# Copying the first output gate out of PSUM, and tying two background steps to the product issued last

## The chip, the cores and the metric

The kernel runs on one core of a Trainium2 chip. The metric is the time on the device in microseconds (us); the reported time is the median of three runs. Next to it stands one execution that the hardware profiler recorded, from which all views of the trace come.

## The reference

One layer of a diffusion backbone, for 256 latent tokens and 256 context tokens of width 2048. Both pass a modulated RMS norm, then one wide input projection `w_in`, whose columns feed two token mixers: attention with 16 query heads on 4 key heads (with a norm and a rotary turn of queries and keys, and a sink), and gated linear attention (GLA) with 4 heads of value width 512. What matters for the change is the attention with its sink, the norm of the keys, and the output gate of the GLA:

```python
def attend_with_sink(parts, sink_g):
    sink_b = sink_g[None, :, :, None]
    m = sink_b
    for s, _ in parts:
        m = jnp.maximum(m, s.max(axis=-1))
    denom = jnp.exp(sink_b - m)
    ...
    for s, val in parts:
        p = jnp.exp(s - m[..., None])
        denom = denom + p.sum(axis=-1)
        o = jnp.einsum("bhgqk,bkhd->bqhgd", p, val.astype(jnp.float32))
        ...
    return out / jnp.transpose(denom, (0, 3, 1, 2))[..., None]
```

The four heads of the GLA's output are normed and multiplied with the SiLU of four blocks of 512 columns of the input projection (the "output gate", RB in the kernel). Both mixers are projected, merged by sigmoid gates (GA and GB), projected again and added to the stream; a gated convolutional FFN follows. All is computed in float32.

## The kernel before

**How a product is made.** Weights stream from HBM in tiles of 256 x 512 (`wload`, seven buffers, on SyncE's DMA queue). Each is split into a high part `whi` (a copy on ScalarE, ACT, into a rounded format, L220) and the rest `wlo` (a subtraction on VectorE, DVE, L221), three buffers of each. Every product is three matmuls on TensorE (PE): high x high, low x high, high x low. The activations are split the same way: `split` (L61 to L63) makes `hi` on ACT and `lo` on DVE. `mm` (L84) issues a matmul of the main stream and remembers it in `last[0]`; `last_lo[0]` is the last `wlo` subtraction. `proj_nat` runs over the rows of a weight block in steps of 256, 12 matmuls a step where two tiles of 128 tokens come out and 24 where four do, into banks of PSUM named `acc` (four banks), and calls `tick()` at the start of each step and `midway()` in the middle. Three more banks are of a kind `side` (names `pg`, `pS`, `ptp`, `poa`, `pto`), one is `main` (`ptk`, `ptq`).

**What sets the order.** The program is written in one stream, and a scheduler places each instruction on its engine's queue; at run time each engine takes its queue in order. Background work (norms, transposes, attention) is put in between by `defer(n, fn)`, which calls `fn` n ticks later, and by a generator `beside`, of which `tick` and `midway` advance a part. `in_order(a, b)` adds a dependency without a semaphore: the scheduler places b behind a in time, and at run time nobody waits for it.

**The first place (456 to 545 us in the trace).** The GLA's value columns of the third and fourth head are not multiplied directly with the tokens; `pair_values` first mixes the tokens. `natural(kp)` takes 256 columns of x and of the context in natural layout (tile `raw`, 128 x 4 x 256), scales them by the norm with four operations on DVE (L1144) with a row tile `rows`, adds the shift (two on POOL or DVE, L1149), splits them into `h0` or `h1` by the parity of kp, and calls `fetch(kp + 1)`, which loads x, context and `rows` of the next; `rows` has one buffer. `inner(kp)` multiplies `h0` or `h1` with the GLA's mixing tiles `ax` and `ac` into two `pg` banks (24 matmuls), and splits them into `h2` or `h3`. `outer(kp, i, w)` multiplies these with the weights. The loop runs inner(0); then natural(2), inner(1), outer(0); natural(3), inner(2), outer(1); and so on to kp = 7. natural(0) and natural(1) are deferred into the product GA before it. The norm and the rotary turn of the keys, `norm_rope(..., copied=True)`, four of them (`keys(i)`), are deferred by 10, 13, 16 and 19 ticks from there; the first step of each is the Square at L1106 on ACT, whose sums DVE takes at L1108. The rotary tables are multiplied by the norm's weights on POOL (L1093 and L1095) in the same stretch.

**The second place (700 to 800 us).** The output gate: `rb_block(j)` computes one block of 512 columns, and `rb_evac` evacuates its two banks with a Silu on ACT (L1336), multiplies it with the normed GLA output on DVE (L1339, L1340), and transposes it later. The attention of the last group of heads runs beside block 0: `attend` puts the scores into banks `pS`, takes exponentials on ACT (L1283), scales them on DVE (L1288), transposes them on PE (`ptp`), splits these (`pth`, `ptl`, L62 and L63) and multiplies them with the values (`poa`). Since exponential and Silu need different tables on ACT, each Silu is tied behind the last exponential, `exps[-1]`, by `in_order`, so that the table is loaded once. Block 2 writes into the banks that block 0 had.

Of the kernel before, what the change touches and what calls it, by code (L numbers as in the profile page):

```python
# [11 lines left out]
AF = mybir.ActivationFunctionType  # L12
# [20 lines left out]
def layer_kernel(ctx, tc, A, out):  # L33
    nc = tc.nc
    V, S, G, PE = nc.vector, nc.scalar, nc.gpsimd, nc.tensor
# [18 lines left out]
    def W2(tag, name, shape, dt=F32):  # L54
        return f2.tile(shape, dt, name=name, tag=tag, bufs=F2_BUFS[tag])
# [5 lines left out]
    def split(hi, lo, src):  # L61
        S.activation(hi, src, AF.Copy)  # L62
        return V.tensor_tensor(lo, src, hi.bitcast(F32), op=ALU.subtract).ins  # L63

    def in_order(*ins):

        for a, b in zip(ins, ins[1:]):
            tc.add_manual_dep(b, a.name, mybir.DependencyInfo(
                mybir.DependencyClass.NoSync, mybir.DependencyReason.DATA), reason="order")

    last, pin = [None], [None]
# [77 lines left out]
    def defer(n, fn):  # L149

        later.append([n, fn])
# [282 lines left out]
    def rms_scale(ss, n, shape):  # L434

        v = sm.tile(shape, F32, name="msq", tag="msq")
        r = sm.tile(shape, F32, name="rstd", tag="rstd")
        t = sm.tile(shape, F32, name="newt", tag="newt")
        V.tensor_scalar(v, ss, 1.0 / n, EPS, op0=ALU.mult, op1=ALU.add)
        S.activation(r, v, AF.Ln)  # L440
        S.activation(r, r, AF.Exp, scale=-0.5)
        V.tensor_tensor(t, r, r, op=ALU.mult)
        V.tensor_tensor(t, t, v, op=ALU.mult)
        V.tensor_scalar(t, t, -0.5, 1.5, op0=ALU.mult, op1=ALU.add)
        V.tensor_tensor(r, r, t, op=ALU.mult)
        return r
# [91 lines left out]
    def affine_shift(s, t0, n, behind=None):  # L538
        for kt in range(t0, t0 + n):
            xk = xr[2 * s + kt // 8][:, kt % 8, :]  # L540
            sh = shift1[:, s, kt:kt + 1]
            hi, lo = hh[kt // 4][:, s, kt % 4, :], hl[kt // 4][:, s, kt % 4, :]
            j = S.activation(hi, xk, AF.Identity, bias=sh).ins
            if behind is not None and kt == t0:
                in_order(behind, j)
            i = V.scalar_tensor_tensor(lo, xk, sh, hi.bitcast(F32), op0=ALU.add, op1=ALU.subtract).ins
        return i, j
# [50 lines left out]
    i, j = affine_shift(0, *groups[0])  # L598
# [3 lines left out]
    for j in range(2):  # L602
        proj_T(w_in, QB + j * 512, kts, [h_all(0)],
               lambda i, b, j=j: evicted.append(S.activation(qb0[2 * j + i], b, AF.Copy).ins), fresh=(j == 0))
# [28 lines left out]
    i, j = affine_shift(1, *groups[1])  # L633
# [341 lines left out]
    def v_block(c0, name, by_tile=False):  # L975
        vh, vl = M(name + "h", [P, 4, 512], F32R), M(name + "l", [P, 4, 512], F32R)
        proj_nat(w_in, 0, c0, ALL, h_xc, lambda i, b: split(vh[:, i, :], vl[:, i, :], b),
                 by_tile=by_tile)
        return vh, vl
# [19 lines left out]
    def with_gla(h, kb, block, extra=()):  # L999
        res, own = [], []  # L1000

        def level():
            if not own:
                own.append(gla_A(h, kb, qbt, *gates[h][0], res))
            next(own[0], None)

        this, following = lambda: gate(h), lambda: gate(h + 1)
        places = {i: [this] for i in ((0, 1, 2, 3) if h == 0 else (0, 1))}
        for i in (4, 6, 7, 8, 9, 10, 11, 12) if h == 0 else (2, 4, 5, 7, 8, 10, 11, 12):
            places[i] = [level]  # L1010
        places.update({13: [level], 14: [following], 15: [level]})
        places.setdefault(13 if h == 0 else 9, []).append(following)

        for i, fn in enumerate(extra):
            places.setdefault(11 + i, []).append(fn)

        def along():
            for i in range(16):
                for fn in places.get(i, ()):
                    fn()  # L1020
                yield

        beside[:] = [along(), 1.0, 0.0]
        v = block()
        for _ in beside[0]:
            pass
        beside.clear()
        return res, v
# [14 lines left out]
    def first_values(i):  # L1043
        if not v:
            v.extend((M("v0h", [P, 4, 512], F32R), M("v0l", [P, 4, 512], F32R)))
        split(v[0][:, i, :], v[1][:, i, :], vb0[:, i, :])

    a, kb1 = with_gla(0, kbt, kb_block, [lambda i=i: first_values(i) for i in range(4)])
    gla_o(0, a, *v)
    defer(2, send_rows)  # L1050
    a, v = with_gla(1, kbt, lambda: v_block(VB + 512, "v1"))
# [16 lines left out]
    def fetch(kp):  # L1068
        if kp >= KT // 2:
            return  # L1070
        raw = wr.tile([P, 4, T], F32, name="raw", tag="raw")
        for s, src in enumerate((A["x"], A["ctx"])):
            load(raw[:, 2 * s:2 * s + 2, :], src[0][:, kp * T:(kp + 1) * T].rearrange("(t p) d -> p t d", p=P))
        rows = f2.tile([P, 4, T], F32, name="rows", tag="mod", bufs=1)
        load(rows, drows[kp].rearrange("r d -> (r d)").partition_broadcast(P))
        fetched[kp] = raw, rows
# [21 lines left out]
    def norm_rope(b, r, t, tag, fold=None, copied=False):  # L1098

        y = W2(tag, "y", [P, 4, P])  # L1100
        b = b.rearrange("p (h d) -> p h d", h=4)
        if not copied:
            S.activation(y, b, AF.Copy)
            b = y
        sq = W2("fc", "sq", [P, 512])
        S.activation(sq, b.rearrange("p h d -> p (h d)"), AF.Square)  # L1106
        s4 = sm.tile([P, 4], F32, name="s4", tag="s4")
        V.tensor_reduce(s4, sq.rearrange("p (h d) -> p h d", h=4), op=ALU.add, axis=AX.X)  # L1108
        z = sq.rearrange("p (h d) -> p h d", h=4)
        if fold is None:  # L1110
            r4 = rms_scale(s4, HD, [P, 4])
            V.tensor_tensor(y, b, r4.unsqueeze(2).to_broadcast([P, 4, P]), op=ALU.mult)
        if r is None:
            V.tensor_tensor(z, y, norms[:, 1:2, :].to_broadcast([P, 4, P]), op=ALU.mult)
            return z
        for u in range(2):
            V.tensor_tensor(z[:, :, u * 64:u * 64 + 64], y[:, :, 64 - u * 64:128 - u * 64],
                            r[:, t, 1:2, u * 64:u * 64 + 64].to_broadcast([P, 4, 64]), op=ALU.mult)
        V.tensor_tensor(y, y, r[:, t, 0:1, :].to_broadcast([P, 4, P]), op=ALU.mult)
        V.tensor_tensor(z, z, y, op=ALU.add)  # L1120
        if fold is not None:
            r4 = rms_scale(s4, HD, [P, 4])
            V.tensor_scalar(fold, r4, SCALE, None, op0=ALU.mult)
        return z
# [16 lines left out]
    def natural(kp):  # L1141
        raw, rows = fetched.pop(kp)
        for i in range(4):
            a = V.scalar_tensor_tensor(raw[:, i, :], raw[:, i, :], rcol[:, i:i + 1], rows[:, i // 2, :],  # L1144
                                       op0=ALU.mult, op1=ALU.mult).ins
            in_order(last_lo[0], a)
            if i % 2:
                x_ = raw[:, i - 1:i + 1, :]
                (V if i == 3 else G).tensor_tensor(x_, x_, rows[:, 2 + i // 2:3 + i // 2, :].to_broadcast([P, 2, T]),  # L1149
                                                   op=ALU.add)  # L1150
        e = kp % 2
        split(hh[e][:, 1], hl[e][:, 1], raw)
        fetch(kp + 1)

    def pair_values():
# [52 lines left out]
        for kp in range(n + 1):  # L1208
            if kp + 1 < n and kp:
                natural(kp + 1)  # L1210
            if kp < n:
                inner(kp)
            if kp:
                for i in range(2):
                    tick()
                    r0 = (kp - 1) * 2 * P
                    outer(kp - 1, i, wsplit(w_in[r0:r0 + 2 * P, VB + (2 + i) * 512:VB + (3 + i) * 512]))
# [114 lines left out]
    def rb_block(j):  # L1332
        def rb_evac(t, b):
            o_ = og[j // 2][:, j % 2, t, :]
            s_ = W2("fc", "sr", [P, 512])
            silu = S.activation(s_, b, AF.Silu).ins  # L1336
            in_order(exps[-1], silu)
            exps.append(silu)
            in_order(silu, V.scalar_tensor_tensor(o_, o_, rg[:, j, t:t + 1], glan, op0=ALU.mult, op1=ALU.mult).ins)  # L1339
            V.tensor_tensor(s_, s_, o_, op=ALU.mult)  # L1340
            defer(4 + t, lambda: to_T(s_, gh, gl, j, t))

        proj_nat(w_in, 0, RB + j * 512, ALL, h_x, rb_evac)
# [19 lines left out]
    for j in range(4):  # L1363
# [6 lines left out]
        def at_evac(t, b, a1=a1, j=j):  # L1370
            if j == 0:
# [5 lines left out]
                 lambda t, b, a2=a2: sig.append(S.activation(a2[t], b, AF.Sigmoid)))  # L1377
# [246 lines left out]
```

## Time and profile before

| what | value |
|---|---|
| median of three runs | 1958.6 us (1956.49 to 1958.75) |
| profiled execution, its own time | 1963.1 us |
| its span, first to last instruction | 1961.3 us |
| mean granted clock of PE | 0.997 |
| instructions | 26490 |
| bytes moved by DMA | 429.26 MB |

The span is what the views show; the 1.8 us beside it lie before the first instruction and behind the last. A row of the timeline has the start in us, the duration in us, the engine, the line of the kernel, the operation and its tiles (out<-in), and in brackets how long the engine had been idle before and what released it. "x4" means four instructions in a row; a matmul's duration includes its way through the array, so that the next starts before it ends. "PEclk" or granted clock is the share of full speed that PE was given.

### The profile page before, as it was taken

How to read it: one execution, taken by the hardware profiler on the slowest of the kernel's cores; microseconds unless marked ns; L12 is line 12 of the kernel's file. 1: busy time of each engine (PE TensorE's matmuls, PEld its weight loads, DVE VectorE, ACT ScalarE, POOL GpSimd, SP SyncE). 2: the span in 40 equal slices, each digit the busy share in tenths (PEclk: the TensorE clock that was granted, in tenths of full speed). 3: DMA queues.
4: the chain of work that ended last, by engine and by line, in shares of the span. 5: the costliest groups of instructions: out<-in, count | busy, mean ns of one | idle time of the engine just before them, and what ended most of it. 6: DMA issues, size and time to landing. Idle time of an engine off the chain costs nothing.

```text
span 1961.3 us, 26490 instructions
## 1 busy us (share of the span) xinstructions
PE 1937.9 (99%) x9906; PEld 1607.7 (82%) x9906; DVE 1440.5 (73%) x2217; ACT 992.8 (51%) x1441; POOL 53.6 (3%) x72
## 2 busy tenths in 40 slices
PE   8999999999999998999999999999999999999999
PEld 6678888887887787888888888888888888888887
DVE  6756867788667888887878567998886545777654
ACT  5224666644356655444444445755565334555533
POOL 0010011011000000000000000000000000000000
PEclk9999999999999999999999999999999999999999
DMA  9984222236554455999999877688886666666663
GB/s 396 412 305 133 76 76 65 81 111 203 156 161 119 139 174 191 323 333 325 326 343 334 304 260 240 197 273 283 274 279 217 194 193 183 184 187 188 192 211 112
DMA packets 188209, 429.26 MB, mean 219 GB/s; under 512 B 12961, under 2 KB 17313, under 8 KB 182833
## 3 DMA queue, kind: packets, MB, share of 16 engines
q1 hardware_dynamic: 186416, 421.84, 64.8%
q0 software_dynamic: 1488, 5.57, 0.9%
q8 instruction: 77, 1.26, 0.3%
q14 instruction: 52, 0.42, 0.1%
q10 hardware_dynamic: 176, 0.17, 0.0%
HBM read 425.37 MB, written 2.16 MB: 218 GB/s over the span
## 4 chain that ended last, share of the span: by engine, by line
PE 95%; DMA 3%; DVE 1%; ACT 1%; issue 0%; SPq 0%; DVEq 0%
PE acc L84 72%; PE accs L84 13%; PE pa L96 2%; PE pg L84 2%; PE poa L96 1%; PE pS L96 1%; DMA mraw<-in_w_mod 1%; PE pm L96 1%; PE ptp L99 1%; DMA xr<-in_ctxT 1%; DMA raw<-in_w_in 1%; PE po L96 1%; PE pto L99 0%; DMA pack<-in_k_pack 0%; ACT s L1283 0%; DMA rows<-drows 0%
## 5 line engine op out<-in xcount | busy, mean ns | idle before, releaser
L220 ACT ACTIVATE whi<-raw 128x1024 fp32r<-128x1024 f32 x568 | 601.4, 1060 | 740.0 <-PE acc L84 579.9
L221 DVE TENSOR_TENSOR wlo<-raw,whi 128x1024 fp32r<-128x1024 f32 x568 | 693.5, 1223 | 357.5 <-ACT whi L220 346.5
L84 PE MATMUL accs<-h,whi 128*128 128x512 f32 x704 | 246.7, 396 | 0.0
L84 PE MATMUL acc<-h,whi 128*128 128x512 f32 x640 | 224.3, 396 | 0.0
L84 PE MATMUL accs<-h,wlo 128*128 128x256 f32 x704 | 196.2, 279 | 0.0
L84 PE MATMUL acc<-h,wlo 128*128 128x256 f32 x640 | 178.3, 279 | 0.0
L84 PEld LDWEIGHTS accs<-h,whi 128*128 128x128 f32 x704 | 132.1, 188 | 31.7
L84 PEld LDWEIGHTS acc<-h,whi 128*128 128x128 f32 x640 | 120.1, 188 | 28.8
L84 PE MATMUL acc<-whi,ah 128*128 128x512 f32 x352 | 137.0, 389 | 0.0
L84 PE MATMUL acc<-whi,al 128*128 128x512 f32 x352 | 136.9, 389 | 0.0
L84 PEld LDWEIGHTS accs<-h,wlo 128*128 128x128 f32 x704 | 132.5, 188 | 0.0
L84 PEld LDWEIGHTS acc<-h,wlo 128*128 128x128 f32 x640 | 120.5, 188 | 0.1
L84 PE MATMUL acc<-whi,h2hi 128*128 128x512 f32 x256 | 101.3, 396 | 0.0
L84 PE MATMUL acc<-whi,th 128*128 128x512 f32 x256 | 100.5, 393 | 0.0
L84 PE MATMUL acc<-whi,h3hi 128*128 128x512 f32 x256 | 100.4, 392 | 0.0
L84 PE MATMUL acc<-whi,h2lo 128*128 128x512 f32 x256 | 99.8, 390 | 0.0
L84 PE MATMUL acc<-whi,h3lo 128*128 128x512 f32 x256 | 99.8, 390 | 0.0
L84 PE MATMUL acc<-whi,tl 128*128 128x512 f32 x256 | 99.7, 389 | 0.0
L84 PE MATMUL acc<-wlo,ah 128*128 128x512 f32 x352 | 94.2, 389 | 0.0
L84 PE MATMUL acc<-whi,h0hi 128*128 128x512 f32 x224 | 88.4, 394 | 5.0 <-ACT sr L1336 5.0
L84 PE MATMUL acc<-whi,h1hi 128*128 128x512 f32 x224 | 88.2, 394 | 0.0
L84 PE MATMUL acc<-whi,h0lo 128*128 128x512 f32 x224 | 87.6, 391 | 0.0
(414 smaller groups left out, 3553.4 us busy)
## 6 DMA issues: line engine op xcount, KB each, us to landing
raw<-in_w_in SPq DMA_DIRECT2D x204, 512.0 KB, 4.4
raw<-in_w_up SPq DMA_DIRECT2D x176, 512.0 KB, 4.1
raw<-in_w_modT SPq DMA_DIRECT2D x128, 512.0 KB, 5.1
raw<-in_w_down SPq DMA_DIRECT2D x88, 512.0 KB, 3.8
mraw<-in_w_mod SPq DMA_DIRECT2D x32, 1024.0 KB, 14.0
raw<-in_w_attn_o SPq DMA_DIRECT2D x32, 512.0 KB, 5.3
raw<-in_w_gla_o SPq DMA_DIRECT2D x32, 512.0 KB, 5.7
raw<-in_w_out SPq DMA_DIRECT2D x32, 512.0 KB, 5.0
```

What stands on the lines that cost most here:

```text
L84: r = pe_seq(PE.matmul(*a, **k))
L96: return pe_seq(after(PE.matmul(*a, **k)))
L99: return pe_seq(after(PE.transpose(*a)))
L220: j = S.activation(hi[:, 0:n, :], raw[:, 0:n, :], AF.Copy).ins
L221: i = V.tensor_tensor(lo[:, 0:n, :], raw[:, 0:n, :], hi[:, 0:n, :].bitcast(F32), op=ALU.subtract).ins
```

## The change

Three edits.

- In `rb_evac`, for block 0 only, the bank is copied on ACT into the SBUF tile `sr`, and the Silu works in place on that copy. The Silu stays behind the last exponential; the copy is not tied to it.
- The Square of the keys' norm (`copied=True` only) is tied behind `last[0]`, the matmul that the main stream issued last.
- Each of the four scalings in `natural` is tied behind `last[0]` as well as behind `last_lo[0]`.

```diff
@@ norm_rope @@
         sq = W2("fc", "sq", [P, 512])
-        S.activation(sq, b.rearrange("p h d -> p (h d)"), AF.Square)
+        i = S.activation(sq, b.rearrange("p h d -> p (h d)"), AF.Square).ins
+        if copied:
+            in_order(last[0], i)
         s4 = sm.tile([P, 4], F32, name="s4", tag="s4")
@@ natural @@
             in_order(last_lo[0], a)
+            in_order(last[0], a)
             if i % 2:
@@ rb_evac @@
             s_ = W2("fc", "sr", [P, 512])
+            if j == 0:
+                S.activation(s_, b, AF.Copy)
+                b = s_
             silu = S.activation(s_, b, AF.Silu).ins
             in_order(exps[-1], silu)
```

In the changed kernel the lines stand a little further down: the scaling L1144 is L1146, the addition L1149 is L1152, the keys' sum L1108 is L1110, the exponentials L1283 are L1286, the new copy is L1340 and the Silu L1336 is L1342.

DVE at the start of `pair_values`, around the first subtractions `h2lo` of inner(0). Before:

```order
L221 TENSOR_TENSOR wlo<-raw,whi 128x1024
L1144 SCALAR_TENSOR_TENSOR raw<-raw,pack,rows 128x256
L221 TENSOR_TENSOR wlo<-raw,whi 128x1024
L1144 SCALAR_TENSOR_TENSOR raw<-raw,pack,rows 128x256 x3
L1108 TENSOR_REDUCE s_4251<-sq 128x4
L1149 TENSOR_TENSOR raw<-raw,rows 128x512
L439 TENSOR_SCALAR msq<-s_4251 128x4
L1108 TENSOR_REDUCE s_4368<-sq 128x4
L1108 TENSOR_REDUCE s_4537<-sq 128x4
L63 TENSOR_TENSOR h2lo<-pg,h2hi 128x512
L63 TENSOR_TENSOR h0lo<-raw,h0hi 128x1024
L63 TENSOR_TENSOR h2lo<-pg,h2hi 128x512
```

And of the change, the same place:

```order
L221 TENSOR_TENSOR wlo<-raw,whi 128x1024 x3
L1146 SCALAR_TENSOR_TENSOR raw<-raw,pack,rows 128x256
L63 TENSOR_TENSOR h2lo<-pg,h2hi 128x512 x2
L1146 SCALAR_TENSOR_TENSOR raw<-raw,pack,rows 128x256 x3
L1152 TENSOR_TENSOR raw<-raw,rows 128x512
L63 TENSOR_TENSOR h0lo<-raw,h0hi 128x1024
L63 TENSOR_TENSOR h3lo<-pg,h3hi 128x512 x2
```

Of natural(2) one scaling is left ahead of the two `h2lo`, and the three sums of the keys' norm now come only after the `h3lo` of inner(1), behind the rows shown. natural(0) and natural(1), whose scalings stood further up, begin some steps later as well; on POOL the multiplications of the rotary tables come ahead of natural(0)'s addition, and on SP the loads of `rows` shift by one or a few weight tiles.

ACT around the last exponentials and the Silu of blocks 0 and 1. Before:

```order
L1283 ACTIVATE s,ds<-s,mx,qr 128x512
L220 ACTIVATE whi<-raw 128x1024
L1283 ACTIVATE s,ds<-s,mx,qr 128x512 x3
L1336 ACT_TABLE_LOAD
L1336 ACTIVATE sr<-acc 128x512 x4
L62 ACTIVATE pth<-ptp 128x512 x4
```

And of the change, first the place some 40 us earlier, where the copies went (`qT` are queries of the last group, `pth` attention weights of its first 128 tokens), then the place shown above:

```order
L62 ACTIVATE qT<-ptq 128x4x128
L441 ACTIVATE rstd<-rstd 128x4
L220 ACTIVATE whi<-raw 128x1024
L1340 ACTIVATE sr<-acc 128x512 x2
L62 ACTIVATE pth<-ptp 128x512 x4
```

```order
L220 ACTIVATE whi<-raw 128x1024
L1286 ACTIVATE s,ds<-s,mx,qr 128x512
L1342 ACT_TABLE_LOAD
L1342 ACTIVATE sr<-sr 128x512
L220 ACTIVATE whi<-raw 128x1024
L1342 ACTIVATE sr<-sr 128x512
L62 ACTIVATE pth<-ptp 128x512
L1342 ACTIVATE sr<-acc 128x512
L220 ACTIVATE whi<-raw 128x1024
L62 ACTIVATE pth<-ptp 128x512
L1342 ACTIVATE sr<-acc 128x512
```

The four Silus no longer stand in one run; the first two read the copies (`sr<-sr`), and weight splits come between the exponentials and the Silus.

PE at the end of block 1 and the start of block 2 (`acc<-whi,h0hi` is block 2's first matmul, `ptp` the transposes of the scaled exponentials of the last 128 tokens). Before:

```order
L84 MATMUL acc<-wlo,h3hi 128x512 x4
L84 MATMUL acc<-whi,h0hi 128x512
L99 MATMUL ptp<-pack,s 128x128 x8
L96 MATMUL poa<-pth,vah 128x512
L96 MATMUL poa<-pth,val 128x512
```

And of the change, from the last four low products of block 2's second step on:

```order
L84 MATMUL acc<-wlo,h0hi 128x512 x4
L84 MATMUL acc<-whi,h1hi 128x512
L84 MATMUL acc<-whi,h1lo 128x512
L84 MATMUL acc<-whi,h1hi 128x512
L84 MATMUL acc<-whi,h1lo 128x512
L84 MATMUL acc<-whi,h1hi 128x512
L99 MATMUL ptp<-pack,s 128x128 x8
```

29 matmuls of block 2 (two whole steps of 12 and five more) now stand ahead of the eight transposes, where one stood.

## The prediction

> **What bounds the kernel now.** I read the page's first part, then PE's waits, then windows, and last the rows of each engine around the two waits that the change can touch. First the page:
>
> ```profile
> PE 1937.9 (99%) x9906; PEld 1607.7 (82%) x9906; DVE 1440.5 (73%) x2217; ACT 992.8 (51%) x1441; POOL 53.6 (3%) x72
> ```
>
> TensorE (PE) works for 1937.9 of 1961.3 us. The change neither adds nor removes a matmul, so it can only win what PE idles, and the clock that PE loses around it. PE's waits (engine, line, what it waited for: us in total, times, longest):
>
> ```profile
> PE acc L84 <- ACT sr L1336: 5.0, 1, 5.0
> PE pg L84 <- DVE h2lo L63: 3.3, 1, 3.3
> PE pm L96 <- DMA mraw<-in_w_mod: 2.7, 4, 1.0
> ```
>
> The first is the Silu of an output gate, the second the split of the first pair product. Nothing else in the list belongs to lines of the change. The windows show what follows each wait and how much room other engines have (columns: window, its length, PE, PEld, DVE, ACT, POOL busy, granted clock, DMA share, GB/s):
>
> ```profile
> 456.00:545.00 89.00, 85.69 (x379) 70.43 (x378) 63.83 (x103) 36.56 (x55) 8.05 (x6) 0.98 0.51 153
> 743.00:757.00 14.00, 8.99 (x40) 7.36 (x40) 12.00 (x22) 9.44 (x18) 0.00 (x0) 0.76 0.45 146
> 950.00:1100.00 150.00, 150.00 (x671) 124.19 (x670) 123.30 (x152) 63.77 (x65) 0.00 (x0) 1.00 0.95 333
> ```
>
> After 757 us PE has no wait on ACT or DVE, and even where DMA is at 0.95 it is busy for 150 of 150 us. A microsecond won earlier should therefore reach the end.
>
> **The first wait, at 462 us.** PE's rows (start, duration, what ran):
>
> ```profile
> 461.29 0.62 PE L84 MATMUL pg<-ax,h1hi 128*128 128x512 f32 x2
> 461.74 0.61 PE L84 MATMUL pg<-ac,h1hi 128*128 128x512 f32 x2
> 465.67 0.74 PE L84 MATMUL pg<-ax,h1hi 128*128 128x512 f32 x2 [3.31 <-DVE h2lo L63]
> 471.97 0.39 PE L84 MATMUL acc<-whi,h2hi 128*128 128x512 f32 x1
> ```
>
> inner(1) writes its first bank with the four matmuls that begin at 461.29 (0.227 us each by the two starts, 0.45 per pair) and needs a second one at 462.20. That is the bank from which DVE still had to make h2lo. The gap is 465.67 - 462.20 = 3.47 us. The other 20 matmuls took 471.97 - 465.67 = 6.30 us where 20 x 0.227 = 4.53 would do: 1.77 us more, at a lower clock. Together **5.24 us**. What DVE did instead:
>
> ```profile
> 458.72 0.48 DVE L1144 SCALAR_TENSOR_TENSOR raw<-raw,pack,rows 128x256 f32<-128x256 f32 x1 [3.88 <-DMA rows<-drows]
> 462.49 0.67 DVE L1108 TENSOR_REDUCE s<-sq 128x4 f32<-128x512 f32 x1
> 463.75 1.26 DVE L1108 TENSOR_REDUCE s<-sq 128x4 f32<-128x512 f32 x2
> 464.94 0.67 DVE L63 TENSOR_TENSOR h2lo<-pg,h2hi 128x512 fp32r<-128x512 f32 x1
> ```
>
> It stood 3.88 us waiting for natural(2)'s rows, then did its scaling and three sums of the keys' norm, and only then h2lo, whose hi half ACT had finished at 461.27 (460.69 + 0.58):
>
> ```profile
> 460.69 0.58 ACT L62 ACTIVATE h2hi<-pg 128x512 fp32r<-128x512 f32 x1
> ```
>
> **Edits 2 and 3 (natural's scaling and the keys' Square behind the last product issued)** add no instruction and no wait at run time; they move the place in each queue. In the new DVE order one scaling of natural(2) stands ahead of the two h2lo, and the keys' sums come behind inner(2). So, walking the queues with the durations of the rows, h2lo runs at about 461.3 to 461.9 (ACT's end, then 0.67), against a need at 462.20: the wait goes, with some 0.3 us to spare. For that, natural(2)'s rows must land before 457.3 or so, where I put that scaling. Their tile has a single buffer, which natural(1) frees; natural(1) moves to about 444 to 448, its load goes out behind it, and with the 4.93 us that the same load took before, the rows land near 453.4. The weight loads that SP holds behind it have seven buffers, so six more steps of 12 matmuls (2.72 us each) are covered. DVE's work from 456 to 545 stays 63.83 of 89 us, with the keys' norms one per two or three steps instead of three at once. Value of both edits: **-5.2 us**; bounds -5.24 and 0 (h2lo late by other DVE work).
>
> On POOL the rope multiplications move ahead of natural(0)'s addition, which today they queue behind:
>
> ```profile
> 425.11 1.46 POOL L1149 TENSOR_TENSOR raw<-raw,rows 128x512 f32<-128x512 f32 x1 [5.56 <-DVE raw L1144]
> 427.09 0.47 POOL L1093 TENSOR_TENSOR att<-rope,norms 128x128 f32<-128x128 f32 x1
> 430.46 0.59 POOL L1095 TENSOR_TENSOR att<-rope,norms 128x64 f32<-128x64 f32 x2
> 427.05 4.30 DVE L1144 SCALAR_TENSOR_TENSOR raw<-raw,pack,rows 128x256 f32<-128x256 f32 x1
> 428.47 1.60 PE L96 MATMUL pa<-q2s,kk 128*128 128x256 f32 x12
> ```
>
> Twelve rope multiplications ran from 427.09 to 431.05 (3.96 us), and one scaling on DVE took 4.30 us beside them, not 0.48. In the new order that scaling is not there; the last splits of the linear attention (ax, kk, q3s, q2s) are, and PE takes q2s from 428.47 on. By walking the queues I put the rope block at about 422.5 to 426.4 and q2s ready some 0.4 us before its first late use: cost 0. If the block began later, q2s could be up to 3.96 - 1.4 = 2.6 us late (1.4 is from the scaling's 427.05 to PE's 428.47), with 1.8 us of clock as above, 4.4 us together. The Trainium skill ("SBUF — State Buffer", section "SBUF: two separate sides") says that DVE and GpSimd share a port pair and that the loser blocks for the whole instruction; the 4.30 us row agrees, and by that rule alone this change trades a blocked scaling that nobody waited for against a split that PE waits for: the second rival below.
>
> **Edit 1 (the first gate copied out of PSUM).** PE and ACT around 743 us:
>
> ```profile
> 741.90 1.07 PE L84 MATMUL acc<-wlo,h3hi 128*128 128x512 f32 x4
> 748.01 0.80 PE L84 MATMUL acc<-whi,h0hi 128*128 128x512 f32 x1 [5.04 <-ACT sr L1336]
> 748.60 1.91 PE L99 MATMUL ptp<-pack,s 128*128 128x128 f32 x8
> 753.89 0.39 PE L96 MATMUL poa<-ptl,vah 128*128 128x512 f32 x1
> 729.55 1.28 PE L99 MATMUL ptp<-pack,s 128*128 128x128 f32 x8
> 745.15 0.80 ACT L1283 ACTIVATE s<-s,mx,qr 128x512 f32<-128x512 f32 x1
> 746.06 1.28 ACT L1336 ACT_TABLE_LOAD   x1
> 747.36 2.07 ACT L1336 ACTIVATE sr<-acc 128x512 f32<-128x512 f32 x4
> ```
>
> RB1's last four matmuls leave PE at 742.80 (741.90 + 4 x 0.227). RB2's first matmul needs RB0's bank, and RB0's Silu is kept behind the attention's last exponential, so it starts at 748.01: 5.21 us. Then 7 matmuls of 512 and 12 transposes took 753.89 - 748.01 = 5.88 us, where 7 x 0.227 + 12 x 0.13 = 3.15 would do (eight transposes took 1.04 us at 729.55, to the next matmul at 730.59): 2.73 us at the lower clock of the window, 0.76. Together **7.94 us**.
>
> With the copy, RB0's banks are free long before, near 707 us, and RB2 goes on at 742.80. Cost of the copies: two ACT operations of 128x512 from PSUM, by the Silu of this shape
>
> ```profile
> L1336 ACT ACTIVATE sr<-acc x8: 575/592/618, 747.4 to 802.6; 128x512 f32<-128x512 f32 x8
> ```
>
> 0.59 us each, 1.2 us. They stand ahead of the four pth splits of attention at 706 us. The order gives PE six RB1 matmuls (1.4 us) between those transposes and the first poa, which hides 1.2 us just so; without the cover PE would lose 1.2 us. I take 0, the cover being whole on paper.
>
> What is late next: after RB2's first 29 matmuls (742.80 + 29 x 0.227 = 749.4) come eight transposes of s, which DVE must have scaled after the exponentials:
>
> ```profile
> 747.09 1.67 DVE L1288 TENSOR_SCALAR s<-s,ds 128x512 f32<-128x512 f32 x4
> ```
>
> Today that ends at 748.76. In the new order one more weight split stands among ACT's exponentials (about 1.0 us) and its lo half on DVE, so I get 750.0 or a little less: a wait of about 0.5 us (bounds 0 and 1.4). A gap of that size costs no clock, by the nearest row:
>
> ```profile
> 18.64 1.07 PE L96 MATMUL pm<-mraw,cS 128*32 128x256 f32 x16 [0.97 <-DMA mraw<-in_w_mod]
> 18.00:22.00 4.00, 3.36 (x35) 2.52 (x36) 2.35 (x8) 2.22 (x5) 0.00 (x0) 1.00 1.03 411
> ```
>
> Here PE waited 0.97 us and the granted clock stayed 1.00. Value: -7.94 + 0.5 = **-7.4 us**; bounds -7.9 and -5.3 (1.4, and the 1.2 of the copies without their cover).
>
> **The clock terms.** They are 1.77 and 2.73 of the sum, read from rows:
>
> ```profile
> 464.00:473.00 9.00, 7.33 (x25) 5.87 (x26) 7.71 (x26) 3.56 (x10) 0.00 (x0) 0.81 0.35 118
> ```
>
> The Trainium skill ("TensorE: Matmul & The Clock Gate", section "Part 1: The HAM clock gate") has half clock after an idle window of about 3.4 us and full clock after as long a busy one; by it each wait would cost about 1.7 us extra, and the sum would be 1 us smaller. The first wait agrees (1.77), the second does not (2.73); the rows decide.
>
> **Sum.** -5.2 - 7.4 = -12.6 us. The profiled execution took 1963.1 us (span 1961.3 and 1.8 around it); 1950.5 after. The runs' median is 1958.6, 4.5 below that execution, and both waits are in every execution as far as one trace can tell: 1958.6 - 12.6 = **1946.0**.
>
> **Rivals.**
> 1. Stage A's wait is only replaced: the slack of 0.3 us at h2lo is short, and a later weight split or natural(2)'s scaling may hold it. Then edit 1 alone is left: 1958.6 - 7.4 = 1951.2. For it: DVE is at 72% there. Against: two h2lo stand nearly alone in the order.
> 2. The rope block holds q2s: 1946.0 + 4.4 = 1950.4. For it, the 4.30 us row; against, 5.56 us in which POOL stood idle before, so it can begin early.
> 3. The Silu's wait is replaced by one on the exponentials or pth, as long and with its clock loss; stage A alone gains: 1958.6 - 5.2 = 1953.4. For it: ACT must still do exponentials, a table load of 1.28 us and four Silus in a row. Against: PE now has 29 matmuls (6.6 us) to do meanwhile.
> 4. The change does not do what it says: both waits pass to the next producer, 1958.6. The order speaks against it, since both blocking instructions are visibly gone from the places where they stood.
> 5. **Slower.** The keys' norm, spread over pair_values, comes in front of inner's splits in four steps instead of once. Its price on DVE:
>
> ```profile
> L1108 DVE TENSOR_REDUCE s<-sq 128x4 f32<-128x512 f32 x12 | 7.8, 675 | 0.0
> L1117 DVE TENSOR_TENSOR sq<-y,att 128x256 f32<-128x256 f32 x20 | 8.0, 416 | 0.0
> L1119 DVE TENSOR_TENSOR y<-y,att 128x512 f32<-128x512 f32 x10 | 6.8, 682 | 0.0
> ```
>
> 0.68 + 2 x 0.42 + three of 0.68 = 3.6 us a norm, and five tiny operations. A step lasts 89/8 = 11.1 us, of which DVE's other work takes (63.8 - 4 x 3.6)/8 = 6.2; so there are 1.3 us to spare in a step with a norm, if nothing stands idle. If each norm stood whole before a split, four steps would be late by up to 3.6 us and 1.8 of clock: 4 x 5.4 = 21.6, and 1946.0 + 21.6 = 1967.6. It turns the sum slower once the mean lateness with its clock loss is over 12.6/4 = 3.2 us a step. Against it: the order sets the norm's operations singly between splits.
>
> **How the numbers follow.** Forecast 0.62, rivals 0.11, 0.06, 0.08, 0.07 and 0.06. The likeliest gives 1946.0. The range runs from 1943.5 (all of both losses gone, 13.2 us, and 2 us for the spread of the median) to 1954.0, which takes in rivals 1 to 3: 0.87 less what falls beyond the edges. A measurement of this kernel tells 0.2% (3.9 us) from no change: faster below 1954.7 (0.86), same to 1962.5 (0.08), slower 0.06.
>
> **What would show it.** Right: no wait of PE on h2lo or sr, the granted clock near 1 in the windows 456 to 545 and 743 to 757, the h2lo subtraction within 1 us of its h2hi, and a wait of PE before the eight transposes of s of 0 to 1.4 us. Wrong, step by step: a wait on pg (rival 1 or 5: see which DVE row stands ahead of the split), on pa near 428 (rival 2), on ptp or poa over 2 us (rival 3). A new wait on weights after 757 us would mean that the gain is given back in the weight stream.

## The result and the profile after

| | median us | lowest to highest |
|---|---|---|
| before, 4 runs beside the change | 1958.45 | 1956.49 to 1958.75 |
| changed kernel, 4 runs | 1945.83 | 1945.76 to 1945.88 |

The ratio is 0.9938, with a 95% interval of 0.992 to 0.9955: 12.6 us faster by the medians, 8.8 to 15.7 by the interval. The profiled execution of the change took 1945.88 us, with a span of 1944.1.

PE's waits after the change, all of them (engine, line, what it waited for: us in total, times, longest):

```profile
PE warm L572 <- DMA pack<-in_k_pack: 6.4, 1, 6.4
PE pm L96 <- DMA mraw<-in_w_mod: 3.3, 6, 1.1
PE acc L84 <- ACT h0hi L543: 0.7, 1, 0.7
```

Both waits that the change could touch are gone, and none has come in their place. The same windows as before the change (window, length, busy time of PE, PEld, DVE, ACT, POOL, granted clock, DMA share, GB/s):

```profile
456.00:545.00 89.00, 89.00 (x402) 73.68 (x401) 70.42 (x110) 40.64 (x64) 11.42 (x7) 1.00 0.56 169
743.00:757.00 14.00, 14.00 (x76) 11.37 (x75) 13.65 (x22) 9.93 (x17) 0.00 (x0) 1.00 0.48 151
```

PE is busy throughout, 402 matmuls where 379 began in the first window and 76 where 40 did in the second, and the granted clock is 1.00 where it was 0.98 and 0.76.

**At the pair products.** PE's rows, then DVE's, from the timeline of the changed kernel:

```profile
461.42 0.62 PE L84 MATMUL pg<-ax,h1hi 128*128 128x512 f32 x2
461.87 0.62 PE L84 MATMUL pg<-ac,h1hi 128*128 128x512 f32 x2
462.32 0.84 PE L84 MATMUL pg<-ax,h1hi 128*128 128x512 f32 x3
466.86 0.39 PE L84 MATMUL acc<-whi,h2hi 128*128 128x512 f32 x1
458.70 0.48 DVE L1146 SCALAR_TENSOR_TENSOR raw<-raw,pack,rows 128x256 f32<-128x256 f32 x1
461.34 0.69 DVE L63 TENSOR_TENSOR h2lo<-pg,h2hi 128x512 fp32r<-128x512 f32 x1 [2.16 <-ACT h2hi L62]
```

The fifth matmul of inner(1) follows the fourth at once, at 462.32, and the whole of inner(1) takes 466.86 - 461.42 = 5.44 us, which is 24 x 0.227. DVE has only the one scaling ahead of h2lo, waits 2.16 us for ACT's half and is done at 462.03, 0.29 us before PE needs the bank.

**At the output gate.** PE, ACT and DVE rows of the changed kernel:

```profile
736.63 1.07 PE L84 MATMUL acc<-wlo,h3hi 128*128 128x512 f32 x4
737.54 0.39 PE L84 MATMUL acc<-whi,h0hi 128*128 128x512 f32 x1
743.88 0.39 PE L84 MATMUL acc<-whi,h1hi 128*128 128x512 f32 x1
744.12 1.34 PE L99 MATMUL ptp<-pack,s 128*128 128x128 f32 x8
700.54 1.06 ACT L1340 ACTIVATE sr<-acc 128x512 f32<-128x512 f32 x2
741.76 1.28 ACT L1342 ACT_TABLE_LOAD   x1
743.07 1.68 DVE L1291 TENSOR_SCALAR s<-s,ds 128x512 f32<-128x512 f32 x4
```

Block 2's first product starts at 737.54, where block 1's last one ends. The Silus now begin after 743.0, and nobody on PE waits for them. The eight transposes start at 744.12, straight behind the product of 743.88, while DVE is still scaling the later heads until 744.75: a transpose waits for its own head only, as the run with half a block copied shows below.

### The profile page after: what moved, and what is told of

Same layout as the page of the kernel before. It is cut to its first block, busy times and chain, and to the rows that moved or that the text cites. A ratio compares the mean times of both kernels' runs of the same rounds, so it can differ in the third digit from the quotient of the medians.

```text
span 1944.1 us, 26485 instructions
## 1 busy us (share of the span) xinstructions
PE 1928.8 (99%) x9906; PEld 1603.9 (83%) x9906; DVE 1436.2 (74%) x2217; ACT 992.2 (51%) x1443; POOL 58.1 (3%) x72
## 3 DMA queue, kind: packets, MB, share of 16 engines
HBM read 425.37 MB, written 2.16 MB: 220 GB/s over the span
## 4 chain that ended last, share of the span: by engine, by line
PE 96%; DMA 3%; DVE 0%; ACT 0%; issue 0%; SPq 0%
PE acc L84 73%; PE accs L84 13%; PE pa L96 2%; PE pg L84 2%; PE poa L96 1%; PE pS L96 1%; DMA mraw<-in_w_mod 1%; PE pm L96 1%; DMA xr<-in_ctxT 1%; PE ptp L99 1%; DMA raw<-in_w_in 1%; PE po L96 1%; PE pto L99 0%; DMA pack<-in_k_pack 0%; PE plr L646 0%; PE pz L96 0%
## 5 line engine op out<-in xcount | busy, mean ns | idle before, releaser
L84 PE MATMUL acc<-whi,h1lo 128*128 128x512 f32 x224 | 87.6, 391 | 0.0
```

The lines of the kernel that those rows point to most:

```text
L84: r = pe_seq(PE.matmul(*a, **k))
```

## The experiments

**Edit 1 alone, and edits 2 and 3 alone.** The first has only these lines, the second only the two `in_order` lines of the change:

```diff
+            if j == 0:
+                S.activation(s_, b, AF.Copy)
+                b = s_
             silu = S.activation(s_, b, AF.Silu).ins
```

> Edit 1 alone. Theory (two separate waits, each undone by its own edit): the 5.2 us gap before RB2's first product and the 2.7 us of lower clock behind it go, the gap at pg stays: 1958.5 - 7.9 = 1950.5 us, a wait of PE on h2lo of about 3.3 us in the trace. Rival (the edits need one another, so that attention and gates come to a different place without the other two): the wait on sr is replaced by one of over 2 us on ptp or poa, 1953 us or more.

> Edits 2 and 3 alone. Theory: the gap of 3.5 us at pg and its 1.8 us of lower clock go, the wait on sr of 5.0 us stays: 1958.5 - 5.2 = 1953.3 us. Rival: natural's later start makes a wait elsewhere in the pair products, 1955 us or more.

Measured: edit 1 alone 1950.35 us (1948.87 to 1951.38), ratio 0.9961 [0.9948, 0.9973]; edits 2 and 3 alone 1953.58 us (1953.13 to 1954.55), ratio 0.9979 [0.997, 0.9987]; the kernel before, beside them, 1957.85 us over 27 runs (1955.85 to 1960.03). That is 7.5 and 4.3 us, together 11.8, where the whole change gave 12.6 against its own runs of before and 12.0 against these. In the trace of edit 1 alone (PE's wait, and its rows around it):

```profile
PE pg L84 <- DVE h2lo L63: 2.8, 1, 2.8
461.23 0.61 PE L84 MATMUL pg<-ax,h1hi 128*128 128x512 f32 x2
465.06 0.72 PE L84 MATMUL pg<-ax,h1hi 128*128 128x512 f32 x2 [2.76 <-DVE h2lo L63]
469.74 0.39 PE L84 MATMUL acc<-whi,h2hi 128*128 128x512 f32 x1
```

No wait on sr, ptp or poa is left; the one at pg stays, with a gap of 465.06 - 462.14 = 2.92 us (four matmuls of 0.227 behind 461.23). In the trace of edits 2 and 3 alone it is the other way round:

```profile
736.58 1.07 PE L84 MATMUL acc<-wlo,h3hi 128*128 128x512 f32 x4
742.70 0.79 PE L84 MATMUL acc<-whi,h0hi 128*128 128x512 f32 x1 [5.05 <-ACT sr L1339]
748.67 0.42 PE L96 MATMUL poa<-ptl,vah 128*128 128x512 f32 x1
```

So the two waits are separate, each edit group undoes its own, and neither rival holds.

**Edit 2 alone and edit 3 alone.**

```diff
 # edit 2
             in_order(last_lo[0], a)
+            in_order(last[0], a)
 # edit 3
+        if copied:
+            in_order(last[0], i)
```

> Edit 2 alone: natural's scalings moved, the keys' sums left where they were. In its order four sums, some dozen tiny operations and one product of the norm stand on DVE ahead of the two h2lo, and none of natural(2). Theory (what holds h2lo is the sum of what stands before it): DVE comes to h2lo at about 463.1 instead of 464.9, so a gap of 1 to 2 us is left of 3.5, with less of the lower clock: 1955 us (1954 to 1956.5). Rival (natural's wait for its rows alone is what held h2lo): no gap, 1953.3 us.

> Edit 3 alone: the keys' norm moved, natural left where it was. Ahead of h2lo stand natural(2)'s first scaling with its wait for the rows until 458.7, a weight split, three scalings and an addition, but no sums. Theory: DVE comes to h2lo at about 463.1, 1.8 us earlier than before: a gap of 1 to 2 us is left, 1955 us (1954 to 1956.5). Rival (the sums alone held it): no gap, 1953.3 us.

Measured: 1954.65 us (1954.05 to 1955.58; ratio 0.9986 [0.9977, 0.9995]) and 1954.66 us (1953.64 to 1955.93; 0.9984 [0.9976, 0.9993]). Of DVE's rows up to the first h2lo, and PE's wait, with edit 2 alone:

```profile
459.63 1.28 DVE L1108 TENSOR_REDUCE s<-sq 128x4 f32<-128x512 f32 x2 [0.27 <-ACT sq L1106]
462.94 0.68 DVE L1112 TENSOR_TENSOR y<-ka,rstd 128x512 f32<-128x512 f32 x1
463.55 1.28 DVE L63 TENSOR_TENSOR h2lo<-pg,h2hi 128x512 fp32r<-128x512 f32 x2
464.28 0.73 PE L84 MATMUL pg<-ax,h1hi 128*128 128x512 f32 x2 [1.35 <-DVE h2lo L63]
```

The keys' norm alone holds h2lo until 463.55. With edit 3 alone:

```profile
458.06 0.49 DVE L1146 SCALAR_TENSOR_TENSOR raw<-raw,pack,rows 128x256 f32<-128x256 f32 x1 [3.25 <-DMA rows<-drows]
459.60 2.31 DVE L1146 SCALAR_TENSOR_TENSOR raw<-raw,pack,rows 128x256 f32<-128x256 f32 x3
462.55 0.68 DVE L63 TENSOR_TENSOR h2lo<-pg,h2hi 128x512 fp32r<-128x512 f32 x1
463.28 0.73 PE L84 MATMUL pg<-ax,h1hi 128*128 128x512 f32 x2 [0.96 <-DVE h2lo L63]
```

natural(2) alone holds it until 462.55. The theory that the work in front adds up stands, and both rivals fall: gaps of 1.51 us (464.28 - 462.77) and 1.11 us (463.28 - 462.17) are left, and only both edits together bring the gap to zero. The price of a gap of 1.1 or 1.5 us, against edits 2 and 3 together, is 1.1 us by the medians (1954.65 and 1954.66 against 1953.58).

**The copies behind the last exponential.** The whole change, with this edit:

```diff
             if j == 0:
-                S.activation(s_, b, AF.Copy)
+                c = S.activation(s_, b, AF.Copy).ins
+                in_order(exps[-1], c)
                 b = s_
```

> The whole change, but the two copies of block 0 are tied behind the last exponential, as the Silu is. In the order the first copy stands right behind the exponentials, the second behind the table load and the first Silu. Theory (what PE waited for is the place behind the exponentials): PE waits 3.5 to 4.2 us at RB2's first product instead of 5.2, with a stretch of lower clock behind it, so 5 to 7 us of edit 1's 7.9 are lost again: 1951 to 1953 us. Rival (the table load and the Silus were the wait): the gap is 2 us or less and without lower clock, 1948 us.

Measured: 1952.18 us (1951.14 to 1952.44), 6.35 us slower than the changed kernel.

```profile
736.79 1.07 PE L84 MATMUL acc<-wlo,h3hi 128*128 128x512 f32 x4
741.49 0.79 PE L84 MATMUL acc<-whi,h0hi 128*128 128x512 f32 x1 [3.63 <-ACT sr L1340]
747.13 0.60 PE L99 MATMUL ptp<-pack,s 128*128 128x128 f32 x4
```

The gap is 741.49 - 737.70 = 3.79 us. From there to the transposes at 747.13, nine matmuls and eight transposes took 5.64 us where 9 x 0.227 + 8 x 0.13 = 3.08 would do: 2.56 more, 3.79 + 2.56 = 6.35 in all, the whole difference. What PE waited for before was thus mainly the place behind the exponentials; table load and Silu were the last 1.4 us of it (5.21 - 3.79). So the copy wins by its early place, not by being cheaper than a Silu.

**Copying two blocks, and copying half a block.** In the first `j == 0` becomes `j < 2`, in the second `j == 0 and t == 0`.

> The whole change, and block 1 is copied out as well (two more copies of 0.59 us on ACT). Theory: nothing of PE waits for block 1's banks, which are needed some 25 us later, so there is nothing to win and ACT has room: 1945.8 us, within 0.5. Rival (ACT is tight between the exponentials and RB2's steps): 1 us or more slower.

> The whole change, but only the first of block 0's two banks is copied; the second waits for its Silu as before. In the order PE has 16 products of RB2's first tile before the eight transposes. Theory: PE works until about 3.6 us later than before edit 1, then waits 1 to 2.5 us for the scaled exponentials or the bank; if the lower clock comes with any wait of 1 us, 3 us or more are lost (1949 us); if it only comes with longer waits, 1 to 2.5 us (1947 to 1948.3 us). Rival (one free bank covers all): 1945.8 us.

Measured: 1946.09 us (1945.97 to 1946.29) with two blocks. That is 0.26 us above the changed kernel, but the two ran in different sets, and against the runs of before beside each the gain is the same 12.6 us (1958.69 - 1946.09 and 1958.45 - 1945.83), so no difference is shown. PE has no wait beyond those at the opening, so ACT had room for two more copies and there was nothing to win. With half a block 1947.23 us (1947.04 to 1947.45), 1.4 us slower:

```profile
741.88 1.68 DVE L1291 TENSOR_SCALAR s<-s,ds 128x512 f32<-128x512 f32 x4
742.42 1.73 PE L99 MATMUL ptp<-pack,s 128*128 128x128 f32 x8 [0.61 <-DVE s L1291]
742.82 0.14 PEld L99 LDWEIGHTS ptp<-pack,s 128*128 128x128 f32 x1 [0.26 <-DVE s L1291]
743.91 0.47 PE L84 MATMUL acc<-whi,h0hi 128*128 128x512 f32 x1
```

PE waits 0.8 us (its last product ended at 741.64), less than the 1 to 2.5 us that were expected. The transposes begin 0.54 us after DVE's scaling began, and not after all four heads, and go on at DVE's pace, with a load for the next head at 742.82; the eight take 1.49 us instead of 1.04. The granted clock of the window 735 to 757 is 1.00. A gap of this size costs little besides itself, and the second free bank is worth having.

**The kernel before, once more.**

> The kernel before, profiled once more. In the first profiled execution of before the pair products of the FFN's up projection stand 0.352 us apart near 1700 us, and its time is 4.5 us above the median. Theory: this belongs to that one execution: here they stand 0.34 us apart, the profiled time is within 1.5 us of 1958.5, and both waits are there again with gaps of 3.5 and 5.2 us. Rival: it belongs to the kernel before, and the change removed it too: 0.352 again.

Measured: 1956.92 us, span 1955.1. The pair products of the FFN (line, operation: lowest/median/highest ns, first and last start), in the first profiled execution and then in this one:

```profile
L84 PE MATMUL accs<-h,whi x704: 392/395/403, 1246.9 to 1847.4; 128*128 128x512 f32 x176
L84 PE MATMUL accs<-h,whi x704: 391/392/395, 1244.9 to 1841.2; 128*128 128x512 f32 x176
```

The stretch took 600.5 us in the one and 596.3 in the other, and every other profiled execution here has the median of 392 ns. The 4.2 us belong to that one execution. Its time here is 1.6 us below 1958.5, just outside what the theory said, and the rows at the two waits tell why. Both gaps are there again:

```profile
461.96 0.61 PE L84 MATMUL pg<-ac,h1hi 128*128 128x512 f32 x2
465.78 0.74 PE L84 MATMUL pg<-ax,h1hi 128*128 128x512 f32 x2 [3.20 <-DVE h2lo L63]
470.48 0.39 PE L84 MATMUL acc<-whi,h2hi 128*128 128x512 f32 x1
740.46 1.07 PE L84 MATMUL acc<-wlo,h3hi 128*128 128x512 f32 x4
746.58 0.79 PE L84 MATMUL acc<-whi,h0hi 128*128 128x512 f32 x1 [5.06 <-ACT sr L1336]
751.72 0.39 PE L96 MATMUL poa<-ptl,vah 128*128 128x512 f32 x1
464.00:473.00 9.00, 7.22 (x32) 5.95 (x33) 9.00 (x27) 4.06 (x11) 0.00 (x0) 1.00 0.37 118
```

3.36 us and 5.21 us. But behind the first gap the 20 matmuls took 470.48 - 465.78 = 4.70 us, only 0.17 too long, at a granted clock of 1.00 where the first execution showed 0.81; behind the second gap 5.14 us instead of 3.15, 1.99 too long instead of 2.73.

**Edit 1 alone, three more executions.** Its five runs spread over 2.5 us, though one gap is all that it has left.

> Edit 1 alone, profiled once more (first of three looks). Its only gap of PE behind the opening is the one at pg, 2.9 us in the first profiled execution, which cost no clock beyond it, yet its five runs spread from 1948.87 to 1951.38. Theory (the gap is near the length at which the clock falls, and the loss comes by chance): over the three looks a gap of 2.9 to 3.5 us each, in one or more of them a loss of 1 to 2 us behind it, and the time moves with gap and loss. Rival (the spread has nothing to do with the gap): the same 2.9 us and 0.15 us each time, while the times differ by over 1 us.

> Edit 1 alone, second of three looks; theory and rival and their numbers as for the first look.

> Edit 1 alone, third of three looks; theory and rival and their numbers as for the first look.

Measured: 1951.52, 1950.84 and 1952.20 us. They are called a, b and c below. Rows of c (the matmul behind the gap and the next stage's first), and DVE's scaling in a:

```profile
465.55 1.22 PE L84 MATMUL pg<-ax,h1hi 128*128 128x512 f32 x2 [3.08 <-DVE h2lo L63]
473.03 0.40 PE L84 MATMUL acc<-whi,h2hi 128*128 128x512 f32 x1
459.11 0.48 DVE L1144 SCALAR_TENSOR_TENSOR raw<-raw,pack,rows 128x256 f32<-128x256 f32 x1 [4.14 <-DMA rows<-drows]
```

The theory holds in its main point and the rival falls: the gap was not the same each time, and time moved with gap and loss. Two figures lay outside what was expected, a's gap of 3.73 us (2.9 to 3.5) and c's loss of 2.95 us (1 to 2). By the same reading as above (the gap, then what the 20 matmuls took beyond 4.53 us):

| profiled execution of edit 1 alone | gap | clock loss | its time | time less both |
|---|---|---|---|---|
| first | 2.92 | 0.15 | 1948.87 | 1945.80 |
| a | 3.73 | 1.74 | 1951.52 | 1946.05 |
| b | 3.20 | 1.72 | 1950.84 | 1945.92 |
| c | 3.24 | 2.95 | 1952.20 | 1946.01 |

Less gap and clock loss, each execution takes what the changed kernel takes, within 0.3 us. The gap's length follows the landing of natural(2)'s rows, for which DVE's scaling waited 3.32 us in the first (it ran at 458.10), 3.61 in b (458.53), 3.65 in c (458.59) and 4.14 in a (459.11). The other kernels close as well: the kernel before, seen again, 1956.92 - 3.36 - 0.17 - 5.21 - 1.99 = 1946.2; late copies 1952.21 - 6.35 = 1945.9; edits 2 and 3 alone 1953.81 - 5.21 - 2.82 = 1945.8; edit 3 alone 1954.14 - 1.11 - 0.16 - 5.21 - 1.84 = 1945.8; edit 2 alone, the furthest off, 1955.58 - 1.51 - 0.14 - 5.20 - 2.22 = 1946.5.

## Why the prediction was right, and where a term was off

- **What bounds the kernel.** PE, its two waits, and the clock behind them: right. Against the second execution of before the sum closes: 3.36 + 0.17 + 5.21 + 1.99 = 10.7 us of loss, and the spans differ by 1955.1 - 1944.1 = 11.0.
- **Edits 2 and 3, -5.2 us.** The mechanism is right: h2lo from 461.34 to 462.03 where 461.3 to 461.9 was forecast, 0.29 us to spare where 0.3 was. The scaling ahead of it ran at 458.70 and not at 457.3, behind a weight split that waited for its tile, which cost nothing, since h2lo waited for ACT anyway. The size was one draw: alone the edits gave 4.3 us by the medians. Gap and clock loss together were 5.24 us in the execution that was read, 3.53 in the second of before, and 3.07, 5.47, 4.92 and 6.19 in the four of edit 1 alone, 4.7 in the mean. The mis-sized term is the clock loss, 0.15 to 2.95 us where one figure of 1.77 was set. Rivals 1 and 5 did not come: there is no wait at pg. One sum of the keys' norm does stand ahead of a split, between the two h2lo of inner(2) (at 478.98) and not behind inner(2) as the prediction had it, and PE did not wait there either. Rival 4 did not come: neither wait passed on to another producer.
- **The rope block on POOL (rival 2).** It did move, to 422.9, and did overlap the last splits:

```profile
422.74 0.43 DVE L63 TENSOR_TENSOR ax<-at,ax 128x256 fp32r<-128x256 f32 x1
422.86 1.83 POOL L1093 TENSOR_TENSOR att<-rope,norms 128x128 f32<-128x128 f32 x1
425.64 2.03 POOL L1095 TENSOR_TENSOR att<-rope,norms 128x64 f32<-128x64 f32 x2
423.67 0.69 DVE L63 TENSOR_TENSOR q3s<-q,q3s 128x512 fp32r<-128x512 f32 x1
425.32 0.91 DVE L63 TENSOR_TENSOR q2s<-q,q2s 128x512 fp32r<-128x512 f32 x1
428.60 1.60 PE L96 MATMUL pa<-q2s,kk 128*128 128x256 f32 x12
```

This time mostly POOL was delayed (1.83 us instead of 0.47, two together 2.03 instead of 0.60), while q2s took 0.91 us where q3s of the same shape took 0.69. q2s was ready at 426.23, 2.4 us before its use; the forecast had 0.4 of slack. It was the forecast's worst-judged margin, on the safe side.

- **Edit 1, -7.4 us.** Alone it gave 7.5. Inside it two terms were off and cancelled: a wait of 0.5 us for the scaled exponentials was put in, and there is none, because each transpose waits for its own head and not for all four (DVE was done 7.2 us after block 1's last product, as forecast). And the clock loss of 2.73 us was on the high side: behind the same gap of 5.2 us it was 1.99 us in the kernel before seen again, 748.67 - 742.70 - 3.15 = 2.82 with edits 2 and 3 alone, 2.22 with edit 2 alone and 1.84 with edit 3 alone, 2.3 in the mean of the five. The copies took 1.06 us on ACT where 1.2 was forecast, and stayed hidden. Rival 3 did not come; the run with the late copies shows what a wait of that kind costs, 6.35 us for a gap of 3.79.
- **The sum.** -12.6 us forecast, -12.6 by the medians; 1946.0 and 1945.83. The agreement to 0.2 us is partly luck: of the two parts run alone one gave 0.9 us less (4.3 against 5.2) and the other 0.1 more, and the medians of before moved between 1957.85 and 1958.69 in three sets of runs.

## What to carry to other kernels

Where a matrix engine is busy nearly all the time, look for its few waits, and for each one look at what stands ahead of the awaited instruction in its own engine's queue: here nothing was too slow, and two operations stood in front of a split that PE needed. A result that must wait for its turn on an engine can be copied out of the bank early, if the copy itself does not wait for that turn; a copy queued at the same late place gave 1.4 of the 7.75 us here (1953.58 without any copy, 1952.18 with the late ones, 1945.83 with the early ones). Count the clock behind a wait as a range and not as one number, and profile the kernel before a second time if much of the sum rests on it: here it was more than a third (1.77 + 2.73 of 12.6).

## What the runs showed of the hardware

The loss of clock behind a gap varied from execution to execution, and so did the time. With no gap, or one of 0.8 us, the runs lay within 0.1 to 0.4 us of each other:

| kernel | gaps of PE, us | lowest to highest, us | runs |
|---|---|---|---|
| changed kernel | none | 1945.76 to 1945.88 | 4 |
| two blocks copied | none | 1945.97 to 1946.29 | 4 |
| half a block copied | 0.8 | 1947.04 to 1947.45 | 4 |
| late copies | 3.8 | 1951.14 to 1952.44 | 6 |
| edits 2 and 3 alone | 5.2 | 1953.13 to 1954.55 | 11 |
| edit 2 alone | 1.5 and 5.2 | 1954.05 to 1955.58 | 11 |
| edit 3 alone | 1.1 and 5.2 | 1953.64 to 1955.93 | 11 |
| edit 1 alone, without a, b and c | 2.9 in the profiled one | 1948.87 to 1951.38 | 5 |
| before | 3.4 and 5.2 | 1955.85 to 1960.03 | 27 |

Behind gaps of 1.1, 1.5 and 2.92 us, and once behind 3.36 us, the matmuls lost 0.14 to 0.17 us beyond the gap and the granted clock stayed at 1.00. Behind the other gaps of 3.2 us and more it fell to 0.50. The windows show this for the first execution of before and for c:

```profile
467.10:470.40 3.30, 3.30 (x10) 2.52 (x9) 3.30 (x20) 0.79 (x5) 0.00 (x0) 0.50 0.49 151
464.80:471.50 6.70, 5.95 (x14) 4.75 (x15) 5.90 (x23) 0.90 (x5) 0.00 (x0) 0.50 0.50 155
```

Windows of 0.2 us give the edges of every such stretch:

| execution | gap, us | PE works again at | clock at 0.50 | its length | half of the part with work | loss measured |
|---|---|---|---|---|---|---|
| edit 1 alone, b | 3.20 | 465.48 | 465.44 to 468.85 | 3.41 | 1.69 | 1.72 |
| edit 1 alone, c | 3.24 | 465.55 | 464.76 to 471.58 | 6.82 | 3.02 | 2.95 |
| before, first | 3.47 | 465.67 | 467.04 to 470.46 | 3.42 | 1.71 | 1.77 |
| edit 1 alone, a | 3.73 | 466.06 | 467.41 to 470.82 | 3.41 | 1.71 | 1.74 |
| late copies | 3.79 | 741.49 | 740.15 to 746.98 | 6.83 | 2.75 | 2.56 |
| edit 2 alone | 5.20 | 745.04 | 742.89 to 749.72 | 6.83 | 2.34 | 2.22 |
| edit 3 alone | 5.21 | 744.00 | 741.02 to 747.85 | 6.83 | 1.93 | 1.84 |
| before, again | 5.21 | 746.58 | 743.94 to 750.77 | 6.83 | 2.10 | 1.99 |
| before, first | 5.21 | 748.01 | 746.94 to 753.76 | 6.82 | 2.88 | 2.73 |
| edits 2 and 3 alone | 5.21 | 742.70 | 741.89 to 748.72 | 6.83 | 3.01 | 2.82 |

A stretch lasted 3.41 us or twice that. It was 3.41 where PE worked through all but 0.04 us of it, and 6.83 where PE was idle for 0.79 us or more of its first half. At half clock matmuls start 0.43 us apart instead of 0.227 ((468.14 - 467.29) / 2 in the first execution of before), so the loss is half of that part of the stretch in which PE had work, within 0.2 us of what was measured. Where the stretch began against the gap differed from execution to execution, even to 1.4 us after PE had started again (467.04 against 465.67); so gaps of one length cost different amounts, and the loss is not a function of the gap.

The Trainium skill ("TensorE: Matmul & The Clock Gate", section "Part 1: The HAM clock gate") has the clock halved after an idle window of about 3.4 us that runs freely, so that its place against the program is chance. The lengths of 3.41 us and the scatter agree with that, and so do the two falls in the first execution of before, which lie 746.94 - 467.04 = 279.90 us apart, 82 times 3.413. The threshold does not: the clock fell behind a gap of 3.20 us, and of the 3.41 us ahead of the fall at 467.04 PE had been idle for 2.04 only (463.63 to 465.67). If the second execution of before has the same spacing, an edge lay at 743.94 - 279.90 = 464.04, which cut its gap of 3.36 us into 1.62 and 1.74, and the clock stayed. By this estimate, from few cases, the limit lies between 1.74 and 2.04 us idle in one window. No run moved the window against the program on purpose.

The two-way block between DVE and POOL is the other finding: in the kernel before a scaling on DVE took 4.30 us beside twelve POOL operations, and after the change a POOL operation took 1.83 us beside three DVE splits in a row, and two together 2.03 beside q2s and a weight split, while the two DVE splits grew by 0.2 and 0.1 us (0.91 for 0.69, 1.34 for 1.22). Which of the two is held was thus not fixed. The Trainium skill ("SBUF — State Buffer", section "SBUF: two separate sides") has the pair of ports go to whichever starts first. The second case agrees (DVE's ax began at 422.74, POOL at 422.86); in the first the recorded starts, 427.05 for DVE and 427.09 for POOL, are too close together to show it.
